# A Winograd convolution on one core: part of the fifth pair's load moves to GpSimd's queue, and one image's separate rows go back to their image

## The chip, the cores and the metric

The kernel runs on one core of a Trainium2 chip. The core has five engines that run side by side: TensorE (PE, matrix products), VectorE (DVE), ScalarE (ACT), GpSimd (POOL) and SyncE (SP, which here only starts transfers). Sixteen DMA engines move data between HBM, where the inputs and outputs lie, and SBUF, the on-chip memory of 128 partitions. A transfer is started by an instruction on an engine's queue; it is cut into packets that the DMA engines work off, and each DMA engine that took part counts up a semaphore when its share has landed.

The metric is device time in microseconds, from the start to the end of one execution. Three runs of the kernel before took 126.76, 126.94 and 127.05 us; their median is 126.94 us.

## The reference

A 3x3 convolution with padding 1, in float32: 16 images of 64 channels and 64 x 64 points, 128 output channels.

```python
output[b, co] += weight[co, ci, kh, kw] * x_pad[b, ci, kh:kh+h, kw:kw+w]
```

summed over the 64 input channels and the nine taps. The input is 16.8 MB and the output 33.6 MB, so 50.3 MB have to pass the DMA engines, beside 0.3 MB of weights.

## The kernel before

**Pairs and halves.** Two images of 64 channels fill the 128 partitions, so the 16 images are eight pairs. `xs[p]` is pair p's input, 16 KB in each partition: partition 64 * b2 + ci holds channel ci of image b2 of the pair. Each pair is computed in two halves of 32 rows, which gives sixteen steps (`halves`). This text counts pairs from one, the code from zero: the fifth pair is `p == 4`, the sixth `p == 5`.

**One step.** The height direction uses a Winograd scheme with fewer products: three transforms of the input are made in float16 (`sums`, `diffs`, `outers`, tiles `ss`, `dd`, `ee`), and ScalarE casts some rows (`cast`, tile `xh`). The transforms of the very first half run on VectorE, all others on GpSimd, two steps ahead of the step that uses them. TensorE multiplies them with transformed weights `Wt` into PSUM tiles (`mms`, `matmul` at L170), ScalarE copies some of these out (L192), and VectorE (L247 to L251) and ScalarE (L253) write the output tiles. After a pair's second half its two output images are stored (`store`).

**Homes.** There are nine places of 16 KB a partition in SBUF, and inputs and outputs share them. `X_HOME` says where a pair's input lies and `O_HOME` where its two output images lie; an output may take a place when the input there has been read, and a later input a place whose reader is done. Places 0 to 4 are single tiles, "b" is a tile of two (outputs of the first, fourth and seventh pair), "d" a tile of two called `two` (inputs of the fourth and fifth, later of the seventh and eighth pair).

**The order on SP's queue.** All transfers are issued by SP in program order, and SP stops at the first whose condition is not met. First come the weights (L59), the first pair in two pieces of rows (0 to 34 and 34 to 64), the second and third pair (L67), and the fourth and fifth pair in one transfer of 4 MB (L81). Then stores and further loads alternate: `NEXT_LOADS` puts the sixth pair's load after the second pair's second half, the seventh's after the fourth pair's first half, the eighth's after the fifth pair's first half. `BOTH` lists the pairs that are stored in one transfer of 4 MB (L207); the others go as two of 2 MB (L216).

**The FEW rows.** For the second image of the sixth pair, `FEW = 5, 1, 7` cuts the last seven rows off: 57 rows go as 128 partitions, the seven rows as one transfer of 124 partitions and one of 4.

```python
if (p, b2) == FEW[:2]:
    at = H - FEW[2]
    parts = [(0, CO, 0, at), (0, 124, at, H), (124, 4, at, H)]
```

**GpSimd's queue** issues no transfers. Its order is: the identity for a transposition, the cast of the weights (L87), and then the transforms, beginning with those of the first pair's second half.

Of the kernel before, what the change touches and what calls it, by code (L numbers as in the profile page):

```python
# [8 lines left out]
F32 = mybir.dt.float32  # L9
# [6 lines left out]
def kernel(  # L16
# [12 lines left out]
    nc = tc.nc  # L29
    B, CI, H, W = x.shape  # L30
    CO = weight.shape[0]
    assert H == 64 and W == 64 and CI == 64 and CO == 128 and B == 16
    NP = B // 2
    RB = 8

    keep = tc.keep_in_program_order
    x_rows = x.rearrange("b c h w -> (b c) h w")
    w_flat = weight.rearrange("co ci kh kw -> co (ci kh kw)")

    const = ctx.enter_context(tc.tile_pool(name="const", bufs=1))  # L40
    psum = ctx.enter_context(tc.tile_pool(name="psum", bufs=8, space=bass.MemoryType.PSUM))
    slots = ctx.enter_context(tc.tile_pool(name="slots", bufs=1))
# [3 lines left out]

    X_HOME = [0, 1, 2, ("d", 0), ("d", 1), 2, ("d", 0), ("d", 1)]
    O_HOME = ["b", (3, 4), (0, 1), "b", (3, 4), (0, 1), "b", (2, 3)]  # L50
    BOTH = (0, 3, 6)
    FEW = 5, 1, 7
    NEXT_LOADS = {(1, 1): 5, (3, 0): 6, (4, 0): 7}

    def home(k, name):
        return slots.tile([128, H, W], F32, tag=f"s{k}", name=name)

    w_raw = const.tile([CO, CI * 9], F32)
    keep(nc.sync.dma_start(w_raw, w_flat))  # L59
    xs = {}  # L60

    def load(p, cuts=((0, H),)):
        if X_HOME[p] in range(5):
            xs[p] = home(X_HOME[p], "xs")
        for lo, hi in cuts:
            keep(
                nc.sync.dma_start(  # L67
                    xs[p][:, lo:hi, :], x_rows[128 * p : 128 * p + 128, lo:hi, :]
                )
            )  # L70

    two = slots.tile([128, 2, H, W], F32, tag="d", name="two")
    for p in range(NP):
        if X_HOME[p] not in range(5):
            xs[p] = two[:, X_HOME[p][1], :, :]

    load(0, ((0, 34), (34, H)))
    load(1)
    load(2)
    rows = x_rows[128 * 3 : 128 * 5, :, :].rearrange("(g p) h w -> p g h w", g=2)  # L80
    keep(nc.sync.dma_start(two, rows))  # L81

    ident = const.tile([128, 128], F16)
    make_identity(nc, ident)

    w16 = const.tile([CO, 2, CI * 9], F16)
    keep(nc.gpsimd.tensor_copy(w16[:, 0, :], w_raw))  # L87
    keep(nc.scalar.copy(w16[:, 1, :], w_raw))

    G0, G1, G2, G21, G01, HP, HM = range(7)  # L90
# [39 lines left out]
    def cast(p, h):  # L130
        t = cpool.tile([128, 17, W], F16, tag="xh", name="xh")
        keep(nc.scalar.copy(t, xs[p][:, C_ROW[h] : C_ROW[h] + 17, :]))  # L132
        return t

    def transforms(eng, p, h):
        return sums(eng, p, h), diffs(eng, p, h), outers(eng, p, h)
# [17 lines left out]
    def mms(tiles, terms, start, stop):  # L154
        n = 3 * len(terms)
        i = 0
        for wi, src, row in terms:
            for kw in (1, 0, 2):
                c_lo, c_hi = max(0, 1 - kw), min(W, W + 1 - kw)
                lo, hi = 0, RB  # L160
                at, step, rows = row
                while at + step * lo < 0:
                    lo += 1
                while at + step * (hi - 1) > rows - 1:
                    hi -= 1
                first, last = at + step * lo, at + step * (hi - 1)
                for b2 in range(2):
                    p0 = 64 * b2
                    keep(
                        nc.tensor.matmul(  # L170
                            tiles[b2][:, lo:hi, c_lo:c_hi],
                            Wt[p0 : p0 + 64, wi, kw, :],
                            src[
                                p0 : p0 + 64,
                                first : last + 1 : step,
                                c_lo + kw - 1 : c_hi + kw - 1,
                            ],
                            start=start and i == 0,
                            stop=stop and i == n - 1,
                            skip_group_check=not start,  # L180
                        )
                    )
                i += 1

    def acc():
        return [psum.tile([128, RB, W], F32, tag="acc", name="acc") for _ in range(2)]

    def copies(tiles):
        us = []
        for b2 in range(2):  # L190
            ut = upool.tile([128, RB, W], F32, tag="ut", name="ut")
            keep(nc.scalar.copy(ut, tiles[b2]))  # L192
            us.append(ut)
        return us
# [1 line left out]
    halves = [(p, h) for p in range(NP) for h in range(2)]  # L196

    def outputs(p):
        if O_HOME[p] == "b":
            both = slots.tile([128, 2, H, W], F32, tag="b", name="both")  # L200
            return both, [both[:, b2, :, :] for b2 in range(2)]
        return None, [home(k, "ot") for k in O_HOME[p]]

    def store(p, both, ots):
        if p in BOTH:
            pair = out[2 * p : 2 * p + 2, :, :, :].rearrange("b c h w -> c b h w")
            keep(nc.sync.dma_start(pair, both))  # L207
            return
        for b2 in range(2):
            parts = [(0, CO, 0, H)]  # L210
            if (p, b2) == FEW[:2]:
                at = H - FEW[2]
                parts = [(0, CO, 0, at), (0, 124, at, H), (124, 4, at, H)]
            for c, n, lo, hi in parts:
                keep(
                    nc.sync.dma_start(  # L216
                        out[2 * p + b2, c : c + n, lo:hi, :], ots[b2][c : c + n, lo:hi, :]
                    )
                )

    for n, (p, h) in enumerate(halves):
        if n + 2 < len(halves):
            tr[halves[n + 2]] = transforms(nc.gpsimd, *halves[n + 2])
        if h == 0:
            both, ots = outputs(p)
            ov = [t.rearrange("p (j i) c -> p j i c", i=2) for t in ots]
        ss, dd, ee = tr.pop((p, h))
        xc = xh.pop((p, h))
        jf, jg = RB * F_BLK[h], RB * G_BLK[h]
        sf, sg = jf - 16 * h, jg - 16 * h  # L230
        g_at = 2 * jg - C_ROW[h]

        pf1, pg1, pf2, pg2 = acc(), acc(), acc(), acc()
        mms(pf1, [(HP, ss, (sf, 1, 16))], True, True)
        ux = copies(pf1)
        mms(pg1, [(G1, ss, (sg, 1, 16))], True, True)
        ug = copies(pg1)
        mms(pf2, [(HM, dd, (0, 1, RB))], True, True)
        uy = copies(pf2)
        if n + 1 < len(halves):  # L240
            xh[halves[n + 1]] = cast(*halves[n + 1])
        mms(pg2, [(G01, xc, (g_at, 2, 17)), (G2, xc, (g_at + 2, 2, 17))], True, True)
        mms(pf1, [(G0, ee, (0, 2, 16))], False, True)
        mms(pg1, [(G21, xc, (g_at + 1, 2, 17)), (G0, xc, (g_at - 1, 2, 17))], False, True)
        mms(pf2, [(G2, ee, (1, 2, 16))], False, True)
        for b2 in range(2):
            keep(nc.vector.tensor_add(ov[b2][:, jg : jg + RB, 1, :], pg2[b2], ug[b2]))  # L247
        for b2 in range(2):
            keep(nc.vector.tensor_add(ov[b2][:, jf : jf + RB, 0, :], pf1[b2], uy[b2]))  # L249
        for b2 in range(2):  # L250
            keep(nc.vector.tensor_sub(ov[b2][:, jf : jf + RB, 1, :], ux[b2], pf2[b2]))  # L251
        for b2 in range(2):
            keep(nc.scalar.copy(ov[b2][:, jg : jg + RB, 0, :], pg1[b2]))  # L253
        if h == 1:
            store(p, both, ots)
        if (p, h) in NEXT_LOADS:
            load(NEXT_LOADS[p, h])


# [28 lines left out]
```

## Time and profile before

| what | us |
|---|---|
| median of three runs | 126.94 |
| profiled execution, its own time | 127.13 |
| its span in the profile | 125.4 |
| TensorE busy | 95.6 |
| GpSimd busy | 90.5 |
| ScalarE busy | 85.4 |
| VectorE busy | 66.8 |
| last matrix product ends at | 102.4 |
| last stores issued at | 103.18 |

Times within the profile count from the start of the span. The page divides the span into 40 slices of 3.1 us and gives for each engine the busy share in tenths; the row "DMA" is the mean busy share of the 16 DMA engines. The queue q1 carries SP's transfers, q8 and q14 carry instructions that the engines fetch while they run. In lists of instructions, a line begins with start and duration, then the engine, the line of the kernel, the operation, and the tile written and read; "SPq" is a transfer issued by SP. What stands in brackets is how long the engine sat idle before, and what ended that.

### The profile page before, as it was taken

The page shows a single profiled execution, that of the slowest core. Times are in us where ns is not written, and L with a number is a line of the kernel's source. Part 1 is how long each engine was busy: PE and PEld are TensorE (multiplying, and loading weights), DVE is VectorE, ACT ScalarE, POOL GpSimd, SP SyncE. Part 2 cuts the span into 40 slices and gives each one's busy share as a digit, 9 for nine tenths or more (in the row PEclk, how much of TensorE's full clock was granted, in tenths as well). Part 3 has the DMA queues.
Part 4 walks back from the last instruction along what each step waited for, and adds up shares of the span by engine and source line. Part 5 has one row for each costly group of instructions (what it writes and reads, how often), then busy time and mean ns, then how long its engine had stood idle before and what let it go on. Part 6 is the DMA issues. An engine that isn't in the chain of part 4 may idle for free.

```text
span 125.4 us, 2343 instructions
## 1 busy us (share of the span) xinstructions
PE 95.6 (76%) x873; PEld 48.9 (39%) x873; DVE 66.8 (53%) x104; ACT 85.4 (68%) x150; POOL 90.5 (72%) x52
## 2 busy tenths in 40 slices
PE   0349999999999999999999999999999960000000
PEld 0223555555455555555555555555555520000000
DVE  0199658393939476574939394765749390000000
ACT  4458598989797988989897979789898930000000
POOL 2209999999999999999999999999999300000000
PEclk9999999999999999999999999999999996555555
DMA  4999999999999999999999999999999999999971
GB/s 132 371 453 423 434 424 439 423 335 418 434 431 429 426 434 418 423 429 434 416 439 424 423 423 423 418 431 434 423 424 423 433 416 443 423 429 444 418 335 47
DMA packets 3827, 50.78 MB, mean 405 GB/s; under 512 B 360, under 2 KB 488, under 8 KB 744
## 3 DMA queue, kind: packets, MB, share of 16 engines
q1 hardware_dynamic: 3816, 50.63, 96.2%
q8 instruction: 7, 0.11, 0.3%
q14 instruction: 4, 0.03, 0.1%
HBM read 17.07 MB, written 33.55 MB: 404 GB/s over the span
## 4 chain that ended last, share of the span: by engine, by line
PE 76%; DMA 2%; DVE 2%; POOL 1%; DVEq 0%; ACT 0%; issue 0%
PE acc L170 75%; DMA w_raw<-in_weight_dram 2%; DVE ss L114 1%; DVE ot L251 1%; POOL w L87 1%; DVEq L283 0%; DVE th L141 0%; DVE Wt L142 0%; PE wp L102 0%; ACT g0h L139 0%; DVEq L142 0%
## 5 line engine op out<-in xcount | busy, mean ns | idle before, releaser
L170 PEld LDWEIGHTS <-Wt 64*128 64x128 f16 x864 | 48.0, 96 | 48.5 <-issue 3.0
L192 ACT COPY ut<-acc 128x512 f32<-128x512 f32 x96 | 48.7, 612 | 4.4 <-PE acc L170 4.4
L170 PE MATMUL acc<-xh,Wt 64*128 64x504 f16 (+3 forms) x384 | 46.2, 372 | 0.0
L170 PE MATMUL acc<-ss,Wt 64*128 64x504 f16 (+1 forms) x192 | 24.8, 392 | 2.3 <-DVE ss L114 2.3
L170 PE MATMUL acc<-ee,Wt 64*128 64x504 f16 (+1 forms) x192 | 26.4, 377 | 0.0
L247 DVE TENSOR_TENSOR ot<-acc,ut 128x512 f32<-128x512 f32 x20 | 12.9, 686 | 20.0 <-ACT ut L192 15.8
L114 POOL TENSOR_TENSOR ss<-xs 128x1024 f16<-128x1024 f32 x7 | 16.6, 2366 | 4.7 <-DMA xs<-in_x_dram 4.7
L127 POOL TENSOR_TENSOR ee<-two 128x1024 f16<-128x1024 f32 x8 | 19.0, 2378 | 0.0
L114 POOL TENSOR_TENSOR ss<-two 128x1024 f16<-128x1024 f32 x8 | 19.0, 2369 | 0.0
L127 POOL TENSOR_TENSOR ee<-xs 128x1024 f16<-128x1024 f32 x7 | 16.6, 2376 | 0.0
L253 ACT COPY ot<-acc 128x512 f32<-128x512 f32 x20 | 10.7, 589 | 5.5 <-PE acc L170 5.5
L170 PE MATMUL acc<-dd,Wt 64*128 64x504 f16 (+1 forms) x96 | 13.9, 392 | 0.0
L247 DVE TENSOR_TENSOR both<-acc,ut 128x512 f32<-128x512 f32 x12 | 7.7, 686 | 11.0 <-ACT ut L192 7.9
L251 DVE TENSOR_TENSOR ot<-ut,acc 128x512 f32<-128x512 f32 x20 | 12.8, 682 | 0.2
L249 DVE TENSOR_TENSOR ot<-acc,ut 128x512 f32<-128x512 f32 x20 | 12.8, 680 | 0.0
L121 POOL TENSOR_TENSOR dd<-two 128x512 f16<-128x512 f32 x8 | 10.3, 1287 | 0.0
L121 POOL TENSOR_TENSOR dd<-xs 128x512 f16<-128x512 f32 x7 | 10.0, 1423 | 0.0
L132 ACT CAST xh<-two 128x1088 f16<-128x1088 f32 x8 | 9.3, 1157 | 0.0
L132 ACT CAST xh<-xs 128x1088 f16<-128x1088 f32 x8 | 9.2, 1145 | 0.0
L253 ACT COPY both<-acc 128x512 f32<-128x512 f32 x12 | 6.4, 589 | 3.5 <-PE acc L170 3.5
L251 DVE TENSOR_TENSOR both<-ut,acc 128x512 f32<-128x512 f32 x12 | 7.7, 683 | 0.1
L249 DVE TENSOR_TENSOR both<-acc,ut 128x512 f32<-128x512 f32 x12 | 7.7, 680 | 0.0
(23 smaller groups left out, 14.9 us busy)
## 6 DMA issues: line engine op xcount, KB each, us to landing
out_dram<-ot SPq DMA_DIRECT2D x9, 2048.0 KB, 18.5
out_dram<-both SPq DMA_DIRECT2D x3, 4096.0 KB, 22.5
xs<-in_x_dram SPq DMA_DIRECT2D x3, 2048.0 KB, 16.2
two<-in_x_dram SPq DMA_DIRECT2D x1, 4096.0 KB, 28.4
two<-in_x_dram SPq DMA_DIRECT2D x2, 2048.0 KB, 23.1
out_dram<-ot SPq DMA_DIRECT2D x1, 1824.0 KB, 24.3
xs<-in_x_dram SPq DMA_DIRECT2D x1, 1088.0 KB, 5.4
xs<-in_x_dram SPq DMA_DIRECT2D x1, 960.0 KB, 7.4
```

The lines of the kernel that those rows point to most:

```text
L87: keep(nc.gpsimd.tensor_copy(w16[:, 0, :], w_raw))
L114: keep(eng.tensor_add(t, v[:, j : j + 16, 0, :], v[:, j : j + 16, 1, :]))
L121: keep(eng.tensor_sub(t, v[:, j : j + RB, 1, :], v[:, j : j + RB, 0, :]))
L127: keep(eng.tensor_sub(t, xs[p][:, r - 1 : r + 15, :], xs[p][:, r + 1 : r + 17, :]))
L132: keep(nc.scalar.copy(t, xs[p][:, C_ROW[h] : C_ROW[h] + 17, :]))
L170: nc.tensor.matmul(tiles[b2][:, lo:hi, c_lo:c_hi], Wt[p0 : p0 + 64, wi, kw, :], src[p0 : p0 + 64, first : last + 1 : step, c_lo + kw - 1 : ...
L192: keep(nc.scalar.copy(ut, tiles[b2]))
L247: keep(nc.vector.tensor_add(ov[b2][:, jg : jg + RB, 1, :], pg2[b2], ug[b2]))
L249: keep(nc.vector.tensor_add(ov[b2][:, jf : jf + RB, 0, :], pf1[b2], uy[b2]))
L251: keep(nc.vector.tensor_sub(ov[b2][:, jf : jf + RB, 1, :], ux[b2], pf2[b2]))
L253: keep(nc.scalar.copy(ov[b2][:, jg : jg + RB, 0, :], pg1[b2]))
```

## The change

All nine homes become one tile, `homes`, and the places keep their numbers (the old "b" is 5 and 6, the old "d" is 7 and 8). Beside that:

- The fourth and fifth pair are loaded by separate transfers. Of the fifth pair, rows 0 to 37 go by SP as 128 partitions. The other 27 rows go by GpSimd's queue for partitions 0 to 119, and by SP in two transfers of four partitions each for 120 to 127.
- GpSimd issues that transfer right after its cast of the weights, between two tiny ones into a tile `spare` that nothing reads: 64 bytes for each of 4 partitions, and for each of 13.
- The FEW rows are gone: the image is stored whole.
- `BOTH` is now the first four pairs; the second and third pair are stored in one transfer, the seventh in two.
- The sixth pair's load stands one half later in the program.

```diff
-    X_HOME = [0, 1, 2, ("d", 0), ("d", 1), 2, ("d", 0), ("d", 1)]
-    O_HOME = ["b", (3, 4), (0, 1), "b", (3, 4), (0, 1), "b", (2, 3)]
-    BOTH = (0, 3, 6)
-    FEW = 5, 1, 7
-    NEXT_LOADS = {(1, 1): 5, (3, 0): 6, (4, 0): 7}
+    X_HOME = [0, 1, 2, 7, 8, 2, 7, 8]
+    O_HOME = [5, 3, 0, 5, 3, 0, 5, 2]
+    BOTH = (0, 1, 2, 3)
+    NEXT_LOADS = {(2, 0): 5, (3, 0): 6, (4, 0): 7}
+    SOFT = 4, 27
+    homes = slots.tile([128, 9, H, W], F32)
+    xs = [homes[:, k, :, :] for k in X_HOME]
...
+    def load(eng, p, lo, hi, c=0, n=128):
+        keep(
+            eng.dma_start(
+                xs[p][c : c + n, lo:hi, :], x_rows[128 * p + c : 128 * p + c + n, lo:hi, :]
             )
-    load(0, ((0, 34), (34, H)))
-    load(1)
-    load(2)
-    rows = x_rows[128 * 3 : 128 * 5, :, :].rearrange("(g p) h w -> p g h w", g=2)
-    keep(nc.sync.dma_start(two, rows))
+        )
+
+    load(nc.sync, 0, 0, 34)
+    load(nc.sync, 0, 34, H)
+    for p in range(1, 4):
+        load(nc.sync, p, 0, H)
+    cut = H - SOFT[1]
+    load(nc.sync, SOFT[0], 0, cut)
+    load(nc.sync, SOFT[0], cut, H, 120, 4)
+    load(nc.sync, SOFT[0], cut, H, 124, 4)
...
     keep(nc.gpsimd.tensor_copy(w16[:, 0, :], w_raw))
+    spare = const.tile([32, 16], F32)
+    keep(nc.gpsimd.dma_start(spare[0:4, :], x_rows[0:4, 0, 0:16]))
+    load(nc.gpsimd, SOFT[0], cut, H, 0, 120)
+    keep(nc.gpsimd.dma_start(spare[4:17, :], x_rows[4:17, 0, 0:16]))
     keep(nc.scalar.copy(w16[:, 1, :], w_raw))
...
         for b2 in range(2):
-            parts = [(0, CO, 0, H)]
-            if (p, b2) == FEW[:2]:
-                at = H - FEW[2]
-                parts = [(0, CO, 0, at), (0, 124, at, H), (124, 4, at, H)]
-            for c, n, lo, hi in parts:
-                keep(
-                    nc.sync.dma_start(
-                        out[2 * p + b2, c : c + n, lo:hi, :], ots[b2][c : c + n, lo:hi, :]
-                    )
-                )
+            keep(nc.sync.dma_start(out[2 * p + b2, :, :, :], ots[b2]))
...
-            load(NEXT_LOADS[p, h])
+            load(nc.sync, NEXT_LOADS[p, h], 0, H)
```

More of the change, by code (lines that the diff above doesn't have):

```diff
@@ L45 @@
     upool = ctx.enter_context(tc.tile_pool(name="upool", bufs=8))
-    X_HOME = [0, 1, 2, ("d", 0), ("d", 1), 2, ("d", 0), ("d", 1)]
-    O_HOME = ["b", (3, 4), (0, 1), "b", (3, 4), (0, 1), "b", (2, 3)]
-    BOTH = (0, 3, 6)
-    FEW = 5, 1, 7
-    NEXT_LOADS = {(1, 1): 5, (3, 0): 6, (4, 0): 7}
-    def home(k, name):
-        return slots.tile([128, H, W], F32, tag=f"s{k}", name=name)
+    X_HOME = [0, 1, 2, 7, 8, 2, 7, 8]
[5 more added lines that the diff above has]
+    xs = [homes[:, k, :, :] for k in X_HOME]
     w_raw = const.tile([CO, CI * 9], F32)
     keep(nc.sync.dma_start(w_raw, w_flat))
[L60 to L65, printed above, removed]
-            keep(
-                nc.sync.dma_start(
-                    xs[p][:, lo:hi, :], x_rows[128 * p : 128 * p + 128, lo:hi, :]
-                )
-            )
[L72 to L75, printed above, removed]
-    load(0, ((0, 34), (34, H)))
-    load(1)
-    load(2)
-    rows = x_rows[128 * 3 : 128 * 5, :, :].rearrange("(g p) h w -> p g h w", g=2)
-    keep(nc.sync.dma_start(two, rows))
+    def load(eng, p, lo, hi, c=0, n=128):
+        keep(
+            eng.dma_start(
+                xs[p][c : c + n, lo:hi, :], x_rows[128 * p + c : 128 * p + c + n, lo:hi, :]
+            )
+        )
[7 more added lines that the diff above has]
+    load(nc.sync, SOFT[0], cut, H, 124, 4)
     ident = const.tile([128, 128], F16)
@@ L198, in outputs @@
     def outputs(p):
[L199 to L202, printed above, removed]
+        both = homes[:, O_HOME[p] : O_HOME[p] + 2, :, :]
+        return both, [both[:, b2, :, :] for b2 in range(2)]
     def store(p, both, ots):
@@ L209, in store @@
         for b2 in range(2):
-            parts = [(0, CO, 0, H)]
-            if (p, b2) == FEW[:2]:
-                at = H - FEW[2]
-                parts = [(0, CO, 0, at), (0, 124, at, H), (124, 4, at, H)]
-            for c, n, lo, hi in parts:
-                keep(
-                    nc.sync.dma_start(
-                        out[2 * p + b2, c : c + n, lo:hi, :], ots[b2][c : c + n, lo:hi, :]
-                    )
-                )
+            keep(nc.sync.dma_start(out[2 * p + b2, :, :, :], ots[b2]))
     for n, (p, h) in enumerate(halves):
```

## The prediction

> **What bounds the kernel now.** I read the page first: engine shares, the 40 slices, the DMA queues, the chain that ended last.
>
> ```profile
> span 125.4 us, 2343 instructions
> ...
> PE 95.6 (76%) x873; PEld 48.9 (39%) x873; DVE 66.8 (53%) x104; ACT 85.4 (68%) x150; POOL 90.5 (72%) x52
> ...
> POOL 2209999999999999999999999999999300000000
> PEclk9999999999999999999999999999999996555555
> DMA  4999999999999999999999999999999999999971
> ...
> q1 hardware_dynamic: 3816, 50.63, 96.2%
> q8 instruction: 7, 0.11, 0.3%
> q14 instruction: 4, 0.03, 0.1%
> ```
>
> The chain blames TensorE (76%), but the slices show TensorE and GpSimd done at four fifths of the span, while the DMA row stands at 9 from the second slice to the 38th. The DMA engines are the bound, and what remains to ask is how they end. Busy time by stretches shows that (DMA share and GB/s are the last two columns).
>
> ```profile
> 110.00:118.00 8.00, 0.00 (x0) 0.00 (x0) 0.00 (x0) 0.00 (x0) 0.00 (x0) 0.50 1.01 432
> ...
> 120.00:121.00 1.00, 0.00 (x0) 0.00 (x0) 0.00 (x0) 0.00 (x0) 0.00 (x0) 0.50 0.77 328
> 121.00:122.00 1.00, 0.00 (x0) 0.00 (x0) 0.00 (x0) 0.00 (x0) 0.00 (x0) 0.50 0.65 279
> 122.00:123.00 1.00, 0.00 (x0) 0.00 (x0) 0.00 (x0) 0.00 (x0) 0.00 (x0) 0.50 0.35 147
> 123.00:124.00 1.00, 0.00 (x0) 0.00 (x0) 0.00 (x0) 0.00 (x0) 0.00 (x0) 0.50 0.08 33
> ```
>
> The share falls from 1.01 to 0.08 over four microseconds: the 16 engines finish one by one, and the slowest sets the time. The trace lists each DMA packet with start, length and size; on an engine the next packet begins 3 to 4 ns before the last ends, so the packets string into 16 chains. These end at 120.17, 120.38, 120.48, 120.74, 121.39, 121.52, 121.97, 122.26, 122.34, 122.59, 122.61, 122.90, 123.20, 123.37, 124.06 and 124.16 us, mean 122.1. Nearly every 16 KB packet takes 611 ns. What sets the chains apart:
> - The chain to 124.06, call it S, has packets of 644 to 662 ns from 36 to 99 us, mostly stores. That costs it some 3.7 us.
> - Each of the seven 16 KB packets of q8 falls on another chain and costs it about 1.4 us (at 34.67 us: 0.93 itself, and the next packet 1.02 in place of 0.61). The four of q14 cost 0.3 to 0.4.
> - The chain to 124.16, call it F, has the first of the seven, at 21.25 us, 1.5 us. So it is still reading when the others begin to store: two packets of 2.15 and 0.77 us at 27 us lose it 1.7 us (most others lose 0.4 to 0.9 there), and the load of the seventh pair costs it 1.1 us more, 6.00 against 4.86.
> - The four chains to 122.59, 122.90, 123.20 and 123.37 carry the FEW rows: 32 packets of 1792 bytes, 74 ns each.
>
> **The change part by part.**
>
> *FEW goes.* Seven rows of one image left 128 partitions evenly (14,592-byte packets, 8 per engine) and went as 124 and 4 partitions, which landed on four engines each. Back with the image, each engine has 8 x 1792 = 14,336 bytes more, at 16,384 bytes in 611 ns 0.535 us. The four lose 2.27 us (first short packet to last landing) and gain 0.535: 1.73 less. S and F are not among the four: S goes to 124.60, F to 124.70.
>
> *The 27 rows.* One partition's 27 rows are 6912 bytes; 8 partitions, an engine's even share, 55,296 bytes or 2.06 us. How 120 partitions spread no row shows. The landings of before do: 128 partitions give 16 increments, 124 give 4, 4 give 4, each the largest number up to 16 that divides the count. By that 120 partitions go to 15 engines, 8 on each, and one engine is left out: 2.06 us less. The other 8 partitions follow on SP's queue as 4 and 4, so on the four engines that FEW used: two more packets each, 0.52 us. The four end at 123.37 - 1.73 + 0.52 = 122.16 at the latest. The remaining eleven or twelve keep their share.
>
> [...]
>
> *Which engine is left out decides nothing by itself.* Left out S: S ends at 122.53, F at 124.70. Left out F: S at 124.60. Left out another: both late. In each case the end moves from 124.16 to 124.6 or 124.7, plus 0.44 to 0.54.
>
> *A second queue on each engine.* The 128 packets interleave with SP's. A row for two queues on one engine is the instruction fetch: 16 KB cost 0.7 to 0.9 us beyond its own 0.61, 8 KB at 36.73 us 0.11 beyond its 0.31. At eight packets an engine that is between 0.1 (once, at entry) and 0.9 us (0.11 each time); a gain has no row, and the engines are at 1.01 already, so I exclude it. I take 0: the data is at rate on either side, and 9472 plus 6912 bytes in two packets cost by the rows (14,592 bytes 545 ns, 7680 bytes 291) about 9 ns more than one of 16 KB. Both ends stay for the range.
>
> *Three issues on GpSimd.* No GpSimd issue is in the trace. SP's take 0.33 to 1.27 us, so three take 1.0 to 3.8. They stand behind the weight cast and ahead of the first sums:
>
> ```profile
> 3.74 0.66 POOL L87 CAST w<-w_raw 128x576 f16<-128x576 f32 x1 [2.44 <-DMA w_raw<-in_weight_dram]
> 9.14 2.35 POOL L114 TENSOR_TENSOR ss<-xs 128x1024 f16<-128x1024 f32 x1 [4.74 <-DMA xs<-in_x_dram]
> ...
> 95.88 2.40 POOL L127 TENSOR_TENSOR ee<-two 128x1024 f16<-128x1024 f32 x1
> ```
>
> The 4.74 us wait covers them. But the 27 rows are read beside the first pair's second piece (8.0 to 8.6 us on the chains), which may come up to 2.06 us later, and GpSimd with it. GpSimd then never catches up; its last tile, done at 98.28, is read by TensorE at 99.64, so 1.36 us are free and compute ends at most 0.7 us late. Even the fastest chain reaches the last pair's stores at 110.4, and they are issued at 103.18: that cover holds. If it went, the delay would count in full.
>
> *The orders on SP.*
>
> ```profile
> 23.24 0.39 SPq L207 DMA_DIRECT2D out_dram<-both  x1
> 34.14 1.85 SPq L216 DMA_DIRECT2D out_dram<-ot  x2
> 39.57 0.34 SPq L67 DMA_DIRECT2D xs<-in_x_dram  x1
> ...
> 92.27 0.41 SPq L207 DMA_DIRECT2D out_dram<-both  x1
> 103.18 1.62 SPq L216 DMA_DIRECT2D out_dram<-ot  x2
> ```
>
> The second and third pairs' stores become one transfer: the first image waits for the second, issued at 34.72. The fastest chain needs it at 37.91, and issue to first packet took 1.0 us for the weights: 2.2 us of cover, which a GpSimd delay of 2 us doesn't reach here, since TensorE has 3 us of slack on GpSimd then. The load of the sixth pair stands one half later, yet it waits for the same last reader (GpSimd's tile that ends at 39.55), with nothing of SP's between. The fourth and fifth pairs load in sequence; the fourth is read first at 39.50, its load landed by 31.2. The four additional early issues at 0.45 us end near 5 us, with the queue full. The seventh pair's split only issues one image earlier. One tile for all nine homes: before, the seventh pair's load went into half of a shared tile at 51.32, as the other half's reads began, so accesses are told apart by range. All at nothing.
>
> Sum: plus 0.54 on the profiled execution's 127.13 (span 125.4), 127.67. That execution is 0.19 above the median of 126.94; on the median, 127.48.
>
> **The rivals.**
> 1. *Faster: S is left out and F's lag was chance.* F's 1.7 and 1.1 us at the changes from loading to storing are not the fetch's own price. The median runs bound F only from above (126.76 means that no chain ended after about 123.8). Were F spared them, it would end near 122, and the next chain (122.61 + 0.535) at 123.15: 1.0 us less, 125.9. The point where it turns faster: F must lose 0.8 us less than in this profile. For it speaks that 2.06 us is just what brings S, 124.06 + 0.54 - 2.06, level with the ordinary chains; against it that F's fetch comes at a fixed point of TensorE's program and its lag meets the same change to stores.
> 2. *No change: S is left out and F loses some 0.3 to 0.8 us less:* 126.7 to 127.2.
> 3. *The second queue costs.* With 0.4 to 0.9 us of interleaving on S or F, 127.9 to 128.4. [...]
> 4. *It does not spread as meant:* fewer than 15 engines carry the 120 partitions. On 8, 15 partitions each, 1.8 us more on some; if S or F were among them, 129.3, otherwise as forecast.
>
> **How the numbers follow.** A difference of 0.2%, 0.25 us, is about what tells from no change here. Forecast (either S or F keeps the end and the 0.54 shows): 0.49, 127.2 to 127.9. Rival 1: 0.26, 125.9 to 126.7. Rival 2: 0.11. Rivals 3 and 4: 0.14. Faster 0.26, same 0.11, slower 0.63. From 126.2 to 128.2 leaves out the better part of rival 1 (about 0.10) and the worse of 3 and 4 (0.07).
>
> **What would show it.** Right: no 1792-byte packets; 128 or so of 6912; one chain without the GpSimd packets, some 2 us ahead of the rest at 30 us; the last landings spread over 3 to 4 us with F or S last; GpSimd's first sums between 9.1 and 11.2; SP's issues where they were. Wrong: the DMA row falling from 9 before slice 37 (starved), a share of 1 until the last two microseconds (levelled, rival 1), or GpSimd's first sums after 12 us.

## The result, and the profile after

The changed kernel takes 131.47 us (median of six runs, 130.42 to 132.49), the kernel before 127.0 us beside it (126.76 to 127.5). The ratio is 1.0332, with a 95% interval from 1.029 to 1.0374: slower by 3.3%, some 4.2 us. It is taken from the averages of the fast runs, without the slow one of 132.49; the medians lie 4.5 us apart. Forecast were 127.5 us and at most 128.2. The profiled execution took 131.53 us with a span of 129.7.

The page of the changed kernel, with the rows that answer to those shown of before:

```profile
span 129.7 us, 2368 instructions
...
PE 97.3 (75%) x873; PEld 49.8 (38%) x873; DVE 67.9 (52%) x104; ACT 85.4 (66%) x150; POOL 92.2 (71%) x55
...
POOL 2708925999999999999999999999999800000000
PEclk9999999999999999999999999999999999655555
DMA  4999999999999999999999999999999999999970
GB/s 123 374 442 260 280 239 358 430 429 407 435 407 435 437 414 435 430 420 435 427 430 420 430 435 414 440 412 420 445 420 420 450 420 422 445 425 425 445 313 20
...
q1 hardware_dynamic: 3696, 49.80, 93.6%
q0 software_dynamic: 208, 0.83, 2.5%
```

The DMA row looks as before: 9 from the second slice to the 38th. The row under it does not. In the fourth, fifth and sixth slice (9.7 to 19.5 us) the engines move 260, 280 and 239 GB/s. The DMA row counts them busy all the while, so the busy share hides the loss. The kernel before has 423, 434 and 424 there. Busy time by stretches, the kernel before and then the changed one (the last two columns are DMA share and GB/s):

```profile
9.00:20.00 11.00, 11.00 (x92) 5.31 (x88) 7.96 (x12) 8.53 (x16) 10.86 (x6) 1.00 1.00 430
```

```profile
9.00:20.00 11.00, 11.00 (x89) 4.79 (x86) 8.76 (x11) 8.24 (x15) 6.89 (x3) 1.00 1.02 266
20.00:24.00 4.00, 2.80 (x28) 1.24 (x26) 3.40 (x6) 2.16 (x4) 3.08 (x2) 1.00 0.98 395
24.00:30.00 6.00, 5.88 (x56) 3.09 (x54) 2.91 (x5) 5.10 (x9) 6.00 (x4) 1.00 0.99 420
```

Over those 11 us, 266 in place of 430 GB/s is (430 - 266) / 430 x 11 = 4.2 us of transfer lost. The 16 chains of packets ended at 122.13 us on average before and end at 126.02 now, 3.9 later; the last ended at 124.16 and ends at 128.27, 4.1 later. So the ends spread about as before, and the whole field has moved. The last chain is now S; F ends at 127.06. The packet records say when: GpSimd's 120 packets of 6912 bytes run from 8.97 to 20.39 us. While they last, a 16 KB packet of SP's queue takes about 1.0 us in the median and up to 1.28, in place of 0.611, and a packet of 6912 bytes 0.39 in the median and up to 0.61, in place of 0.262.

GpSimd's and TensorE's queues feel it, in the timelines of GpSimd and of TensorE of the changed kernel:

```profile
4.38 0.68 POOL L85 DMA_DIRECT2D spare<-in_x_dram  x1
5.05 0.54 POOL L62 DMA_DIRECT2D homes<-in_x_dram  x1
5.58 0.51 POOL L87 DMA_DIRECT2D spare<-in_x_dram  x1
10.19 2.35 POOL L114 TENSOR_TENSOR ss<-homes 128x1024 f16<-128x1024 f32 x1 [4.11 <-DMA homes<-in_x_dram]
...
20.91 2.36 POOL L114 TENSOR_TENSOR ss<-homes 128x1024 f16<-128x1024 f32 x1 [3.83 <-DMA homes<-in_x_dram]
```

```profile
23.33 1.47 PE L170 MATMUL acc<-ss,Wt 64*128 64x512 f16 x12 [1.20 <-POOL ss L114]
```

The three issues cost GpSimd 1.73 us inside its first wait. Its second wait is new: 3.83 us for the second pair's load, and TensorE then waits 1.20 us for GpSimd. Compute ends at 106.05 us, still 22 us before the last packet, and the DMA engines move 427 GB/s from 36 to 112 us, so this is not what sets the time.

### The profile page after: what moved, and what is told of

Its sections match the earlier page's. It is cut to its first block, busy times and chain, and to the rows that moved or that the text cites. A ratio compares the mean times of both kernels' runs of the same rounds, so it can differ in the third digit from the quotient of the medians.

```text
span 129.7 us, 2368 instructions
## 1 busy us (share of the span) xinstructions
PE 97.3 (75%) x873; PEld 49.8 (38%) x873; DVE 67.9 (52%) x104; ACT 85.4 (66%) x150; POOL 92.2 (71%) x55
## 4 chain that ended last, share of the span: by engine, by line
PE 61%; DMA 14%; POOL 5%; SPq 1%; DVEq 1%; issue 0%; DVE 0%
PE acc L170 61%; DMA homes<-in_x_dram 14%; POOL ss L114 2%; POOL ee L127 2%; POOL dd L121 1%; DVEq L272 1%; SPq L62 1%; SPq L58 0%; DVE homes L240 0%
## 5 line engine op out<-in xcount | busy, mean ns | idle before, releaser
L114 POOL TENSOR_TENSOR ss<-homes 128x1024 f16<-128x1024 f32 x15 | 35.4, 2359 | 7.9 <-DMA homes<-in_x_dram 7.9
L236 DVE TENSOR_TENSOR homes<-acc,ut 128x512 f32<-128x512 f32 x32 | 20.6, 686 | 31.3 <-ACT ut L192 21.5
L127 POOL TENSOR_TENSOR ee<-homes 128x1024 f16<-128x1024 f32 x15 | 35.3, 2351 | 0.0
L242 ACT COPY homes<-acc 128x512 f32<-128x512 f32 x32 | 17.2, 588 | 10.4 <-PE acc L170 10.4
L240 DVE TENSOR_TENSOR homes<-ut,acc 128x512 f32<-128x512 f32 x32 | 20.6, 683 | 2.1 <-PE acc L170 1.9
L238 DVE TENSOR_TENSOR homes<-acc,ut 128x512 f32<-128x512 f32 x32 | 20.4, 680 | 0.0
L121 POOL TENSOR_TENSOR dd<-homes 128x512 f16<-128x512 f32 x15 | 20.0, 1334 | 0.0
L132 ACT CAST xh<-homes 128x1088 f16<-128x1088 f32 x16 | 18.4, 1147 | 0.8 <-DMA homes<-in_x_dram 0.8
L102 PE MATMUL wp<-ident,w 128*128 128x128 f16 x9 | 1.1, 309 | 4.6 <-POOL w L80 4.6
L127 DVE TENSOR_TENSOR ee<-homes 128x1024 f16<-128x1024 f32 x1 | 3.4, 3355 | 0.0
L114 DVE TENSOR_TENSOR ss<-homes 128x1024 f16<-128x1024 f32 x1 | 1.2, 1226 | 0.3 <-DMA homes<-in_x_dram 0.3
```

The lines of the kernel that those rows point to most:

```text
L102: keep(nc.tensor.matmul(wp[:, k * CO : k * CO + CO], w16[:, :, 3 * kh + k :: 9], ident))
L114: keep(eng.tensor_add(t, v[:, j : j + 16, 0, :], v[:, j : j + 16, 1, :]))
L121: keep(eng.tensor_sub(t, v[:, j : j + RB, 1, :], v[:, j : j + RB, 0, :]))
L127: keep(eng.tensor_sub(t, xs[p][:, r - 1 : r + 15, :], xs[p][:, r + 1 : r + 17, :]))
```

## The experiments

Three theories were held against each other at first. Q: any second queue beside SP's slows both. G: only GpSimd's own transfers do. E: the uneven spread of the 120 partitions over the DMA engines does, whoever issues them. When the first runs had spoken for the spread, E split into P (the dealing, that is which partitions each engine gets, makes engines meet at the same group of SBUF partitions), D (15 engines, or one left out, are slow as such) and H (the addresses read in HBM). Ratios below are to the kernel before, with 95% intervals.

**sp_piece: the piece by SP's queue.**

```diff
     load(nc.sync, SOFT[0], cut, H, 124, 4)
+    load(nc.sync, SOFT[0], cut, H, 0, 120)
...
-    spare = const.tile([32, 16], F32)
-    keep(nc.gpsimd.dma_start(spare[0:4, :], x_rows[0:4, 0, 0:16]))
-    load(nc.gpsimd, SOFT[0], cut, H, 0, 120)
-    keep(nc.gpsimd.dma_start(spare[4:17, :], x_rows[4:17, 0, 0:16]))
```

> The changed kernel, but the 27 rows of 120 partitions go by SP's queue, right behind the two pieces of four partitions, and the two tiny transfers are gone; GpSimd issues nothing. Theory Q (a second queue of any kind, beside SP's on the same DMA engines, slows both as long as both read): 127.2 to 127.8 us, the reads at 420 GB/s from 9 to 20 us. Theory G (only transfers that GpSimd issues slow the others): the same 127.2 to 127.8. Theory E (the uneven spread over 15 engines and four costs the time, whoever issues it): 130.5 to 131.5.

Measured: 129.22 us, 1.0132 (1.0067 to 1.0196). None of the three: too slow for Q and G, too fast for E. The reads from 9 to 20 us were back at 432 GB/s, but where the piece itself moved, behind the other loads, the rate fell as low as in the changed kernel:

```profile
26.00:30.00 4.00, 4.00 (x41) 2.06 (x38) 2.75 (x5) 3.34 (x7) 4.00 (x2) 1.00 1.02 234
```

In the same four microseconds whole_pair, the same kernel without the split (below), moves 324, since its change from loads to stores falls there. So the piece is slow in one queue too, but only part of the fall to 234 is its own. Its packets show it by themselves: 6912 bytes take 0.50 us in the median. The chains end at 123.54 on average, 1.3 later than in whole_pair (122.24).

**act_piece: the piece by ScalarE's queue.**

```diff
     keep(nc.scalar.copy(w16[:, 1, :], w_raw))
+    load(nc.scalar, SOFT[0], cut, H, 0, 120)
```

and GpSimd's three lines gone.

> The changed kernel, but the 27 rows of 120 partitions are issued by ScalarE, right after its cast of the weights, some 4.5 us into the span, and the tiny transfers are gone. Q: 130.5 to 131.5 us with 260 to 280 GB/s for some 10 us. G: 127.2 to 127.8. E: 130.5 to 131.5.

Measured: 130.67 us, 1.0267 (1.0203 to 1.0331), with 240 to 280 GB/s from 9 to 16 us. G falls: ScalarE's transfer does nearly the same harm as GpSimd's.

**gp_128: GpSimd's transfer with all 128 partitions.**

```diff
-    load(nc.sync, SOFT[0], cut, H, 120, 4)
-    load(nc.sync, SOFT[0], cut, H, 124, 4)
...
-    load(nc.gpsimd, SOFT[0], cut, H, 0, 120)
+    load(nc.gpsimd, SOFT[0], cut, H, 0, 128)
```

> The changed kernel, but GpSimd's transfer of the 27 rows has all 128 partitions, so every DMA engine gets the same share, and SP's two pieces of four partitions are gone; the tiny transfers stay. Q and G: 130.5 to 131.7 us, since the second queue reads as long as before. E: 127.2 to 127.8.

Measured: 128.31 us, 1.0100 (1.007 to 1.013). Nearly the same bytes by the same second queue at the same time, and the stretch is at full rate:

```profile
9.00:20.00 11.00, 11.00 (x96) 4.86 (x93) 8.76 (x12) 8.88 (x16) 10.50 (x6) 1.00 1.01 430
```

Its packets of 6912 bytes took 0.262 us, each one of them. Q falls: two queues that read side by side cost no bandwidth by themselves here. The chains end at 122.15 on average, as before (122.13). The time lies above E's 127.2 to 127.8. What is left over before is in the main the missing FEW rows (next run). Against whole_pair, 127.75 us in another session, some 0.5 us more remain; what they are stays open.

**no_few: the kernel before with the FEW rows back in their image.**

```diff
-    FEW = 5, 1, 7
+    FEW = 9, 1, 7
```

> The kernel before with nothing but the FEW rows undone: the sixth pair's second image is stored whole. All theories, by the prediction's term for FEW: 0.4 to 0.55 us slower than before, 127.4 to 127.6 us, with S and F last and the four engines that carried the short packets 1.7 us earlier. If the prediction's reading of the ends is wrong, within 0.15 us of before.

Measured: 127.77 us, 1.0048 (1.0014 to 1.0082), that is 0.6 us, with an interval from 0.2 to 1.0. The mean end is 122.11, as before; the last two chains end at 124.41 and 124.86 (before 124.06 and 124.16), and the third last at 122.68. The last one has the first instruction fetch, at 21.20 us, as F had.

**whole_pair: the change without the split.**

```diff
-    load(nc.sync, SOFT[0], 0, cut)
-    load(nc.sync, SOFT[0], cut, H, 120, 4)
-    load(nc.sync, SOFT[0], cut, H, 124, 4)
+    load(nc.sync, SOFT[0], 0, H)
```

and GpSimd's three lines gone.

> The changed kernel without the split: the fifth pair goes whole by SP's queue, nothing by GpSimd's, the FEW rows stay with their image. All that is left of the change is the one tile of homes, the merged and split stores, the separate loads and FEW. By the prediction's terms as no_few, 127.5 to 128.0 us, with one dip near 27 us. If the restructuring costs something by itself, over 128.3.

Measured: 127.75 us, 1.0052 (1.0035 to 1.0069), as no_few. One tile for the homes, merged and split stores and the separate loads cost nothing that shows.

**sp_halves: two transfers of 64 partitions by SP's queue.**

```diff
-    load(nc.sync, SOFT[0], cut, H, 120, 4)
-    load(nc.sync, SOFT[0], cut, H, 124, 4)
+    load(nc.sync, SOFT[0], cut, H, 0, 64)
+    load(nc.sync, SOFT[0], cut, H, 64, 64)
```

and GpSimd's three lines gone.

> [...] Theory P (the dealing lets two engines write at a time to partitions that in a whole 128-partition transfer belong to one engine, and such a group of partitions takes no more than one engine's rate): 200 to 240 GB/s while they move, some 2 us lost, 129 to 129.6 us. Theory D (15 engines, or the left-out one, are what slows): full rate, 127.5 to 128. Theory H (the addresses read in HBM): full rate, since the 16 engines together read the same stretch in order as a whole transfer does.

Measured: 128.95 us, 1.0127 (1.0065 to 1.0189), as slow as sp_piece with an even share for every engine. The stretch in which the two move:

```profile
27.00:30.00 3.00, 3.00 (x32) 1.55 (x30) 2.42 (x4) 2.34 (x6) 3.00 (x2) 1.00 1.06 249
```

D falls, and so does H as far as it expected full rate here. With each packet's bytes spread over its duration, the four microseconds from 26 to 30 us have 268, 214, 238 and 228 GB/s. whole_pair has 303, 238, 353 and 419 there, so the first two are mostly its change from loads to stores, and the last two are the piece: about half of 430. Its packets of 6912 bytes take 0.50 us in the median.

**sp_dense: the 120 partitions from a dense stretch of HBM.** 

```diff
+    dense = x.rearrange("b c h w -> (b c h w)")[0 : 120 * 27 * W]
+    keep(
+        nc.sync.dma_start(
+            xs[SOFT[0]][0:120, cut:H, :].rearrange("p h w -> p (h w)"),
+            dense.rearrange("(p n) -> p n", p=120),
+        )
+    )
```

and GpSimd's three lines gone.

> As sp_piece, but the 120-partition transfer reads one dense stretch of HBM, 6912 bytes after 6912 bytes, in place of rows that lie 16 KB apart; the fifth pair is computed from wrong rows. P and D: 128.8 to 129.6 us, with 220 to 260 GB/s while it moves. H: 127.5 to 128, at 420 GB/s.

Measured: 129.16 us, 1.0157 (1.007 to 1.0244), and 253 GB/s from 27 to 30 us; the packets take 0.50 us in the median, as in sp_piece. Other addresses in HBM, the same loss: H falls.

**sp_112: 112 and 16 partitions.**

```diff
-    load(nc.sync, SOFT[0], cut, H, 120, 4)
-    load(nc.sync, SOFT[0], cut, H, 124, 4)
+    load(nc.sync, SOFT[0], cut, H, 0, 112)
+    load(nc.sync, SOFT[0], cut, H, 112, 16)
```

and GpSimd's three lines gone.

> [...] P: the larger at 340 GB/s or more, 127.6 to 128.3 us. D: as fast, 127.5 to 128. A theory that anything but 128 partitions is slow: 129 to 129.6.

Measured: 128.24 us, 1.0107 (1.0068 to 1.0146). Here sp_112 and then whole_pair, which has its change from loads to stores there:

```profile
27.00:30.00 3.00, 3.00 (x32) 1.55 (x30) 2.43 (x4) 2.34 (x6) 3.00 (x2) 1.00 1.00 335
```

```profile
27.00:30.00 3.00, 3.00 (x32) 1.57 (x30) 1.29 (x3) 2.78 (x6) 3.00 (x3) 1.00 0.86 328
```

A packet of 6912 bytes takes 0.33 us in the median, between the 0.26 of gp_128 and the 0.50 of sp_halves. A transfer of 112 partitions does far less harm than one of 120 (0.50 in sp_piece) or 64. P expected that; why it is so, no packet shows.

**gp_halves: GpSimd's transfer as two of 64 partitions.**

```diff
-    load(nc.gpsimd, SOFT[0], cut, H, 0, 120)
+    load(nc.gpsimd, SOFT[0], cut, H, 0, 64)
+    load(nc.gpsimd, SOFT[0], cut, H, 64, 64)
```

and SP's two pieces of four partitions gone.

> As gp_128, but GpSimd's 27 rows go as two transfers of 64 partitions. Theory P (engines that meet at the same group of partitions): as the changed kernel, 260 to 300 GB/s for some 10 us, 130 to 131.7 us, although all 16 engines get the same share. Theory D (15 engines): as gp_128, 128.0 to 128.6 us.

Measured: 131.94 us, 1.0374 (1.0353 to 1.0395), as slow as the changed kernel or a little slower:

```profile
9.00:20.00 11.00, 10.69 (x90) 5.24 (x91) 7.30 (x13) 8.47 (x17) 5.91 (x3) 1.00 1.01 263
```

Against gp_128 the same bytes move in the same queue at the same time, with even shares, and only the halving differs. It makes 430 GB/s into 263. So what costs the time is how many partitions a transfer has. Of the theories only P is left; that the number decides which partitions each engine gets, and that the engines meet at a group of SBUF partitions, is its reason, and no packet shows it.

**rows_13: half of the rows.**

```diff
-    SOFT = 4, 27
+    SOFT = 4, 13
```

> The changed kernel with 13 rows in place of 27 in the split. P: the slow stretch lasts for eight packets an engine all the same, since each waits its turn behind a 16 KB packet, but the shorter packets collide for less time: 129 to 130.3 us. If the loss goes by bytes alone, half of the 3.4 us between the changed kernel and gp_128: 129.7 to 130.1.

Measured: 129.45 us, 1.0192 (1.0137 to 1.0247). The two halves of the stretch show that the slow part lasts half as long:

```profile
9.00:15.00 6.00, 5.75 (x40) 2.59 (x41) 4.04 (x8) 4.52 (x9) 2.45 (x2) 1.00 1.00 292
15.00:20.00 5.00, 5.00 (x52) 2.54 (x48) 3.06 (x6) 3.74 (x9) 5.00 (x3) 1.00 1.00 423
```

Over whole_pair the 27 rows cost 131.47 - 127.75 = 3.7 us and the 13 rows 1.7: by bytes, about. The eight packets an engine that were expected did not come: GpSimd's queue put two partitions into a packet, 60 of 6656 bytes in all, so each engine had four.

**id_after and id_plain: who is left out.** Marker loads of 2 to 15 partitions tell the chains apart: a chain takes some of them and not others. id_after is the changed kernel with four of them behind the first loads and eight at the very end.

```diff
+    mark = const.tile([16, 16, 64], F32)
+    keep(nc.sync.dma_start(mark[0:7, 8, :], x_rows[0:7, 0, :]))
+    keep(nc.sync.dma_start(mark[0:3, 9, :], x_rows[0:3, 0, :]))
+    keep(nc.sync.dma_start(mark[0:5, 10, :], x_rows[0:5, 0, :]))
+    keep(nc.sync.dma_start(mark[0:13, 11, :], x_rows[0:13, 0, :]))
...
+    keep(nc.sync.dma_start(mark[0:2, 0, :], x_rows[0:2, 0, :]))
...
+    keep(nc.sync.dma_start(mark[0:15, 7, :], x_rows[0:15, 0, :]))
```

> [...] Time as the changed kernel's, within 1 us. If the left-out engine is the steady slow one, S, the chain without GpSimd's large packets and the one with packets of 644 to 662 ns are one; my reading of the changed kernel's landings says they are two, the left-out one about 1 us ahead of the others at the end and S about 2 us behind the quickest.

Measured: 133.55 us in a single run, two more than the changed kernel and so over the 1 us expected. The chain that is ahead after the loads (its share of the fifth pair ends at 29.30 us, the next one's at 30.88) takes none of the markers up to 13 partitions. The chain with the packets of 644 to 662 ns ends last, at 128.04, and takes five of the seven end markers that follow at once, those of 6 to 14 partitions. So S and the left-out chain are two.

id_plain drops the two tiny transfers and has markers of 13, 14 and 15 partitions.

> [...] Time as the changed kernel's within 1 us.

Measured: 131.1 us in a single run. The chain ahead ends its share at 29.80 us and takes none of the three. In both runs, with the tiny transfers in front and without them, the left-out chain takes no marker of up to 13 partitions. That fits tiny transfers that don't change which engine is left out; two single runs don't show that it is the same one.

## Why the prediction was wrong, point by point

The direction was forecast rightly, but only some 0.6 us of the slowdown came from the reason given, FEW. That the larger part went the same way was luck.

*What bounds the kernel* held: the DMA engines do, and compute that ended 3 us later cost nothing. But the prediction read the bound from the busy share and let every engine carry its bytes at 611 ns for 16 KB whatever the others did. While the piece moved, SP's packets took about 1.0 us.

*The 27 rows* is the step that failed, in "The remaining eleven or twelve keep their share", together with *a second queue on each engine*, where 0 was taken and 0.9 us was the upper end. Beside the piece none of the engines kept to its 611 ns, and the cost is 3.7 us (changed kernel against whole_pair), or 3.2 against gp_128. The row that the bound came from, an instruction fetch beside a store, is no row for it: a second queue by itself took no bandwidth (gp_128, 430 GB/s). The cost goes with the number of partitions in a transfer. Here the transfer of 128 ran at full rate (gp_128, 0.262 us a packet) and the one of 112 lost a little (sp_112, 0.33); one of 120 and two of 64 ran at about half of it in SP's queue (0.50 us a packet), the 120 from scattered and from dense HBM alike. Beside SP's loads, the 120 by GpSimd's queue pulled the rate of both queues together down to 266 GB/s from 9 to 20 us, the two of 64 by GpSimd's to 263, and the 120 by ScalarE's to between 240 and 280 from 9 to 16 us.

Why just these numbers of partitions are slow, no run shows. That they decide which partitions each engine gets, and that engines then meet at a group of SBUF partitions, is argued, not shown, since packets carry no partition.

The price grew when the piece went beside other loads: 1.3 us of mean end in one queue, 3.8 (126.02 - 122.24) when it alternated with SP's packets. A 16 KB packet of SP's took about 1.0 us in the median then, though it belonged to a whole transfer, and in gp_128 it took 0.611 beside the same bytes. The piece took 11 us to get through in turns, and for all of that time SP's bytes were held up too. By what means one queue's packets slow the other's stays open.

*FEW goes* held: 0.44 to 0.54 us forecast, 0.6 measured (0.2 to 1.0), and the two late chains moved by 0.35 and 0.7 us. Mean ends show what FEW is: it moves no mean, only the last.

*Which engine is left out decides nothing by itself* held: the left-out engine was not S (id_after), and S and F are the last two again (128.27 and 127.06). The relief of 2.06 us was there, 1.7 us at the loads' landings, on an engine that nobody waited for.

*Three issues on GpSimd* and *the orders on SP* held: 1.73 us in a range of 1.0 to 3.8; first sums at 10.19, between 9.1 and 11.2; nothing of the rest shows (whole_pair is as no_few). The second pair's load was not thought of: GpSimd waited 3.83 us for it, and what hung on GpSimd came later, as the sixth pair's load, issued at 44.46 in place of 39.57. With the DMA engines the bound, that cost nothing that shows.

*The rivals.* Rivals 1 and 2 needed S to be the engine left out, and it was not. Rival 1 also rested on F's lag being chance. It is not: no_few has the chain with the first fetch last again, at 124.86, and so do whole_pair (125.09) and gp_128 (124.94). Rival 3 pointed at the right stretch, with the wrong cause and at most a quarter of the size. None of the signs given for a wrong forecast came: GB/s fell under a DMA row of nines, and no sign looked at GB/s.

## What to carry to other kernels

Read GB/s beside the DMA busy share: here the engines counted as busy at 266 GB/s as at 430. A transfer that is meant to balance bytes over DMA engines can cost more than it saves by its number of partitions: here 5% of the input's bytes held up the loads beside them for 11 us. Where rows must be split off, keep all 128 partitions in the transfer (430 GB/s in gp_128, against 266), or measure the rate while the odd one moves.

## What the runs showed of the hardware that was not expected

Two queues of loads on the same DMA engines, one of them GpSimd's, ran at 430 GB/s together, as one does alone. The same 6912 bytes took a DMA engine 0.26 us in a transfer of 128 partitions (gp_128), and in SP's queue 0.33 in the median in one of 112 (sp_112) and 0.50 in one of 120 (sp_piece) or 64 (sp_halves). One DMA engine, whose chain took the end markers of 6 to 14 partitions in id_after, takes 644 to 662 ns for a 16 KB packet from 36 us until compute ends, with and without transfers by GpSimd; why that one stays open. The kernel before, no_few and whole_pair have a dip to 238 to 260 GB/s from 27 to 28 us (each packet's bytes spread over its duration), where loads give way to stores; its cause was not tried.
